# A two-layer decoder step: embeddings split during down, and low halves of gate weights by adding transfers

## Chip, cores and metric

The kernel runs on one core of a Trainium2 chip. The metric is device time of one execution in microseconds (us), as the median of several runs. A profile of one more execution shows where the time goes; times within it count from the start of its span.

## The reference

One inference step of a decoder trunk with two layers, for 512 prompt rows and 8 sample rows (520 columns in all), width 1024. Layer 0 mixes with a short gated convolution, layer 1 with windowed attention on one shared K/V. After the mixer each layer has a feed-forward part and then adds a gated embedding:

```python
hf = rmsnorm(h, norm_ffn_g[i])
h = h + (jax.nn.silu(hf @ ffn_w_gate[i]) * (hf @ ffn_w_up[i])) @ ffn_w_down[i]
gate = jax.nn.sigmoid(rmsnorm(h, norm_ple_g[i]) @ ple_w_gate[i])
h = h + gate * (p[i].astype(h.dtype) @ ple_w_proj[i])
```

Everything is float32. `p[i]` is the layer's embedding input (256 wide), `ple_w_gate` is 1024 x 1024 and `ple_w_proj` 256 x 1024.

## The kernel before

Activations lie feature-major: 8 tiles `h[k]` of 128 features by 520 columns. TensorE multiplies in a fast float format with fewer mantissa bits, so each operand x is split into a high half (ScalarE copies it into that format) and a low half x - high (VectorE subtracts), and each product is three matmuls: high x high, high x low, low x high, on two column halves of 260.

Weights come in raw tiles of 128 x 8 x 128 (512 KB) through SyncE's (SP's) queue into a ring of three raw buffers (`wr`, tag `raw`), in the order of the program. `wsplit` turns each half of a raw tile (four 128-blocks) into a pair of high and low, either in a ring of four pair buffers or in a place given as `dst`. A raw buffer is free when its last reader is done. Where a tile is laid and when an engine takes up an instruction follow from the program order, readiness and free buffers, decided once when the kernel is built; each engine then works in that fixed order.

The feed-forward part (`ffn`) has a plain part of gate and up, then a part in which 2 x 2 blocks are multiplied with seven products instead of eight (`gate_up`, `seven`), then down: a plain part (row blocks m = 0 to 7, 18 weight blocks each, L617 to L628) and a seven-product part (`dd` = 0, 1). In the seven-product parts some low halves are made without VectorE already: `low(..., dma=True)` lets ScalarE write minus the source, rounded to the fast format (that is minus the high half), and a transfer issued on GpSimd's (POOL's) queue adds the source to it (L420 to L424). Down's operands lie in places D7 to D10, DP and X0 to X3, its weight sums in D3 and D4. The two seven-product passes of down end with `after`, which makes squares for the norm (`Norm`) and the operand pairs `px` of the embedding gate: pairs 0 to 3 in D5 and D6, pairs 4 to 7 in X4 to X7. Then the embedding input is loaded and split into `pe` (L649 to L654), in DP.

In layer 0 the gate tiles `pg0{i}` (`dense`, weights through the pair ring) alternate with projection tiles `pj0{m}` (L668 to L682); the norm's factor is finished at `MID` (L670). In layer 1 `last(c, mid)` does the gates and projections once for each column half c. For c = 0 it loads and splits the weights as it goes (`load_last`): projections `wj`, gates 0 and 1 in pair buffers, gates 2 to 7 in D3, D4, D7, D8, D9, D10; for c = 1 they stay there. A gate's bank is freed when VectorE has scaled it by the norm's factor `nq.r` (L1077); that factor comes from a column sum on TensorE, some 13 small VectorE operations (`Norm.start`, `newton_`), a spread by TensorE and a copy by ScalarE (`Norm.spread`, L285). Three banks rotate among gates and projections, and projections lag the gates by two.

Of the kernel before, what the change touches and what calls it, by code (L numbers as in the profile page):

```python
# [10 lines left out]
F32 = mybir.dt.float32  # L11
# [10 lines left out]
T = S + NB  # L22
# [37 lines left out]
def _program(nc, a, o):  # L60
# [3 lines left out]
    with tile.TileContext(nc) as tc, ExitStack() as ctx:  # L64
# [32 lines left out]
        def slot(tag, shape, dt, name):  # L97
            return ap.tile(shape, dt, tag=tag, name=name)
# [30 lines left out]
        def xpair(i, name):  # L129
            t = slot(f"X{i}", [128, 2, T], F32R, name)  # L130
            return t[:, 0, :], t[:, 1, :]
# [20 lines left out]
            V.scalar_tensor_tensor(pair[1], h[k], gain(n, k), pair[0].bitcast(F32), ALU.mult, ALU.subtract)  # L152


        def wsplit(w, name, step=8, dst=None):

            kt = w.shape[1]
            res = []
            for k0 in range(0, kt, step):
                n = min(step, kt - k0)  # L160
                raw = wr.tile([128, 8, 128], F32, tag="raw", name=f"{name}r{k0}")
                nc.sync.dma_start(raw[:, :n], w[:, k0:k0 + n, :])
                for q0 in range(0, n, 4):
                    q = min(4, n - q0)
                    if dst is None:
                        pr = wp.tile([128, 2, 4, 128], F32R, tag="pair", name=f"{name}p{k0 + q0}")
                    else:
                        pr = dst[:, :, k0 + q0:k0 + q0 + q]
                    A.copy(pr[:, 0, :q], raw[:, q0:q0 + q])
                    V.tensor_tensor(pr[:, 1, :q], raw[:, q0:q0 + q], pr[:, 0, :q].bitcast(F32), ALU.subtract)  # L170
                    res += [(pr[:, 0, i, :], pr[:, 1, i, :]) for i in range(q)]
            return res

# [243 lines left out]
            split(4, t4, "D10", True)  # L417
            yield res

        def low(dst, src, hi, dma=False):  # L420

            if dma:
                A.mul(dst, src, -1.0)  # L423
                G.dma_start(out=dst, in_=src, accum_op=ALU.add)  # L424
            else:
                V.tensor_tensor(dst, src, hi.bitcast(F32), ALU.subtract)  # L426

        rings = {"raw": (("raw",) * 3 + ("E0", "E1", "E2"), []), "pair": (("pair",) * 4 + ("E3",), [])}

        def ring(kind, shape, dt, name):  # L430
# [139 lines left out]
        def ffn(i, fx, nf):  # L570

            hid, w = [], {}
            ops = operands(i, nf)
            ahead = weights(a["w_gu"][i], f"{i}", w, ("D3", "DP"), {1: "E4", 3: "E5"})
            plain = [(a[f"w_{n}"][i, m], f"{n[0]}{i}{m}") for m in range(NP) for n in ("gate", "up")]
            mid = [{MID: nf.start}, {4: nf.spread}]
            ws, ps, xs = wsplit(*plain[0]), [], None
            for j in range(2 * NP):
                wn = wsplit(*plain[j + 1]) if j + 1 < 2 * NP else None
                if wn is None:  # L580
                    for _ in range(2):
                        next(ahead)
                ps.append(dense(None, fx, plain[j][1], mid[j] if j < 2 else None, ws))
                ws = wn
                if j % 2:
                    m = j // 2
                    t, u = temp(f"tg{i}{m}"), temp(f"tu{i}{m}")
                    V.tensor_tensor(halves(t), ps[j - 1], halves(nf.r), ALU.mult)
                    A.activation(t, t, AF.Silu)
                    V.tensor_tensor(halves(u), ps[j], halves(nf.r), ALU.mult)  # L590
                    hid.append(cp.tile([128, T], F32, tag=("tabc", "tabs", "k32", "r2")[m], name=f"hid{i}{m}"))
                    V.tensor_tensor(hid[m], t, u, ALU.mult)
                for _ in range((0, 2, 1, 1, 2, 1, 0, 0)[j]):
                    xs = next(ops)
            couples = []
            for d in range(ND):
                if d:
                    t = slot(f"X{d - 1}", [128, 2, T], F32, f"hid{i}d{d}")
                    couples.append(t)
                    out = [t[:, 0], t[:, 1]]  # L600
                else:
                    out = [cp.tile([128, T], F32, tag=tag, name=f"hid{i}{tag}") for tag in ("acc", "r")]
                gate_up(i, d, xs, w, ahead, out)
                hid += out
            hid2, ws = [], []
            for j, tag in enumerate(("D3", "E0", "E1", "E2", "D4", "D5", "D6", "E3", "E4", "E5")):
                if j in (0, 4):
                    ws += wsplit(a["w_down"][i, 0, :, 2 * j:min(2 * j + 8, FP)], f"d{i}0{j}")
                nw = 1 if tag[0] == "E" else 2
                t = slot(tag, [128, nw, 2, T], F32R, f"hid{i}{tag}")  # L610
                for q in range(nw):
                    hid2.append((t[:, q, 0, :], t[:, q, 1, :]))
                    split_to(hid2[-1], hid[len(hid2) - 1])
            ops = inner_operands(i, couples[4:6], couples[6:8])
            w = {}
            ahead = weights(a["w_dd"][i], f"d{i}", w, ("D3", "D4"), {0: "X4", 1: "E4", 3: "E5"})
            for m in range(KD):  # L617
                if m == 2:
                    preload(AF.Sigmoid, h[0])
                if m:  # L620
                    ws = wsplit(a["w_down"][i, m], f"d{i}{m}")
                if m == KD - 1:
                    next(ahead)
                    next(ahead)
                pd = dense(None, hid2, f"d{i}{m}", ws=ws)
                V.tensor_tensor(halves(h[m]), halves(h[m]), pd, ALU.add)
                if m in (2, 4):
                    xs = next(ops)  # L628
            nq = Norm(f"q{i}")
            nid, pairs = (N_PLE0, N_PLE1)[i], []  # L630

            for dd in range(2):
                if dd == 0:
                    for tag in ("D5", "D6"):
                        t = slot(tag, [128, 2, 2, T], F32R, f"px{i}{tag}")
                        pairs += [(t[:, q, 0, :], t[:, q, 1, :]) for q in range(2)]
                else:
                    pairs += [xpair(k, f"px{i}{k}") for k in range(4, KD)]

                def done(x, t, half):  # L640
                    for e in range(2):
                        m = 4 * dd + 2 * e + t
                        c = h[m][:, half * TH:(half + 1) * TH]
                        V.tensor_tensor(c, c, x[:, e], ALU.add)
                        if (t, half) in ((0, 1), (1, 0)):
                            after(m, nq, (nid,), (pairs,))

                seven(f"d{i}", dd, xs, w, ahead, done)
            dp = slot("DP", [128, KP, 2, T], F32R, f"p{i}")  # L649
            pe = [(dp[:, q, 0, :], dp[:, q, 1, :]) for q in range(KP)]  # L650
            for q in range(KP):
                pt = temp(f"pt{i}{q}")
                nc.sync.dma_start(pt, a["pT"][i, :, q, :])
                split_to(pe[q], pt)  # L654
            return pairs, pe, nq

        fx = [xpair(k, f"fx0{k}") for k in range(KD)]
# [9 lines left out]
        pg = {}  # L667
        for i in range(KD + 1):  # L668
            if i < KD:
                pg[i] = dense(a["w_pgate"][0, i], px, f"pg0{i}", {MID: nq.finish} if i == 0 else None)  # L670
                if i == 0:
                    pg[i] = to_sbuf(pg[i], "pg00s")
            m = i - 1
            if m < 0:
                continue
            t = temp(f"tq0{m}")
            V.tensor_tensor(halves(t), pg[m], halves(nq.r), ALU.mult)
            A.activation(t, t, AF.Sigmoid)
            pj = dense(a["w_proj"][0, m], pe, f"pj0{m}")
            V.tensor_tensor(halves(t), pj, halves(t), ALU.mult)  # L680
            V.tensor_tensor(h[m], h[m], t, ALU.add)
            after(m, nk, (N_KV,), (kx,))  # L682
# [358 lines left out]
        def load_last(m):  # L1041
            if m % 2 == 0:
                t = slot(DTAGS[m // 2], [128, 2, 2, KP, 128], F32R, f"wj{m}")
                for q in range(2):
                    wsplit(a["w_proj"][1, m + q], f"wj{m + q}", dst=t[:, q])
                    wj.append([(t[:, q, 0, k], t[:, q, 1, k]) for k in range(KP)])
            if m < 2:
                wg.append(wsplit(a["w_pgate"][1, m], f"wg{m}"))
            else:
                t = slot(("D3", "D4", "D7", "D8", "D9", "D10")[m - 2], [128, 2, KD, 128], F32R, f"wg{m}")  # L1050
                wg.append([(t[:, 0, k], t[:, 1, k]) for k in range(KD)])
                wsplit(a["w_pgate"][1, m], f"wg{m}", dst=t)

        def out_y(ny):
            for k in range(0, KD, 2):
# [139 lines left out]
```

## Time and profile before

| | us |
|---|---|
| median of 3 runs | 1235.31 |
| lowest, highest | 1232.91, 1235.59 |
| the profiled execution | 1235.11 |
| its span | 1233.3 |
| TensorE busy | 1206.2 |
| VectorE busy | 881.1 |
| ScalarE busy | 626.1 |
| GpSimd busy | 106.6 |

The mean granted TensorE clock is 0.99 of full speed. TensorE's instructions overlap, so its busy time says where it had work, and the waits say where it had none. A wait is named by what ended it: the engine, the line and the tile. In the rows a tile's name stands with its number left out where several are alike, and `out<-in` is what an instruction writes and reads.

### The profile page before, as it was taken

What the parts mean: (1) busy time and instruction counts of PE and PEld (TensorE: products, weight loads), DVE (VectorE), ACT (ScalarE), POOL (GpSimd) and SP (SyncE); (2) the same over time, 40 slices, a digit from 0 to 9 for tenths busy, and PEclk for the clock granted to TensorE, in tenths of its full rate; (3) what the DMA queues carried; (4) which work ended last, traced back from release to release, by engine and by line L of the source; (5) the groups of instructions that cost most, each with busy time, mean ns of one, the idle gap of its engine ahead of it and who ended that gap; (6) DMA issues with size and microseconds to landing.
All of it is one profiled execution on the core that took longest, in us unless ns stands there. A gap on an engine that the chain in (4) does not pass through costs nothing.

```text
span 1233.3 us, 23936 instructions
## 1 busy us (share of the span) xinstructions
PE 1206.2 (98%) x9805; PEld 1189.2 (96%) x9805; DVE 881.1 (71%) x1523; ACT 626.1 (51%) x1068; POOL 106.6 (9%) x147
## 2 busy tenths in 40 slices
PE   9999999999999999999998989999999999999896
PEld 8999999999999999999998979999999999999896
DVE  6845557786868853689887777787686779338865
ACT  6322344555555832565544777554555566227531
POOL 2000000101010000100043321000100000001000
PEclk9999999999999999999998999999999999999998
DMA  6223223856565333732431121356656643356312
GB/s 216 87 89 100 89 90 117 206 154 153 155 154 133 83 107 100 204 104 86 146 112 52 41 89 53 117 129 176 154 155 153 159 99 92 94 157 163 108 39 70
DMA packets 56862, 147.59 MB, mean 120 GB/s; under 512 B 5680, under 2 KB 21040, under 8 KB 56752
## 3 DMA queue, kind: packets, MB, share of 16 engines
q1 hardware_dynamic: 47296, 117.66, 30.2%
q0 software_dynamic: 9312, 28.36, 12.4%
q8 instruction: 77, 1.26, 0.4%
q14 instruction: 33, 0.27, 0.1%
q10 hardware_dynamic: 144, 0.03, 0.0%
HBM read 113.10 MB, written 4.58 MB: 95 GB/s over the span
## 4 chain that ended last, share of the span: by engine, by line
PE 88%; DVE 7%; ACT 1%; DMA 1%; issue 1%; POOL 1%; SPq 0%; DVEq 0%; ACTq 0%; POOLq 0%
PE pb L499 13%; PE d L178 13%; PE pd L499 9%; PE pa L499 8%; PE o L178 4%; PE po L178 4%; PE g L178 4%; PE u L178 4%; PE pc L178 3%; PE pg L203 3%; PE pb L178 3%; PE px L178 3%; PE pbd L499 3%; PE pg L178 3%; PE pdd L499 2%; PE pad L499 2%
## 5 line engine op out<-in xcount | busy, mean ns | idle before, releaser
L499 PE MATMUL pb<-xs,wh 128*128 128x260 f32 x864 | 158.9, 283 | 0.0
L499 PEld LDWEIGHTS pb<-xs,wh 128*128 128x128 f32 x864 | 133.4, 188 | 0.0
L426 DVE TENSOR_TENSOR wl<-s,wh 128x1024 fp32r<-128x1024 f32 x72 | 88.1, 1223 | 37.1 <-PE pb L499 27.4
L449 ACT CAST wh<-s 128x1024 fp32r<-128x1024 f32 x72 | 75.7, 1051 | 73.0 <-PE pd L499 53.7
L499 PE MATMUL pd<-xs,wh 128*128 128x260 f32 x576 | 106.9, 286 | 0.0
L499 PE MATMUL pa<-xs,wh 128*128 128x260 f32 x576 | 105.3, 283 | 0.0
L499 PEld LDWEIGHTS pd<-xs,wh 128*128 128x128 f32 x576 | 88.6, 188 | 1.5
L499 PEld LDWEIGHTS pa<-xs,wh 128*128 128x128 f32 x576 | 88.8, 188 | 0.0
L499 PE MATMUL pb<-xs,wl 128*128 128x260 f32 x288 | 81.5, 283 | 0.0
L499 PE MATMUL pd<-xs,wl 128*128 128x260 f32 x288 | 81.4, 283 | 0.0
L499 PEld LDWEIGHTS pd<-xs,wl 128*128 128x128 f32 x288 | 54.2, 188 | 0.0
L499 PEld LDWEIGHTS pb<-xs,wl 128*128 128x128 f32 x288 | 54.2, 188 | 0.0
L499 PE MATMUL pa<-xs,wlE 128*128 128x260 f32 x144 | 40.7, 283 | 0.0
L499 PE MATMUL pa<-xs,wl 128*128 128x260 f32 x144 | 40.7, 283 | 0.0
L499 PE MATMUL pb<-xs,wlE 128*128 128x260 f32 x144 | 40.6, 282 | 0.0
L508 DVE TENSOR_TENSOR u<-pd,u 128x520 f32<-128x520 f32 x36 | 25.0, 695 | 21.7 <-PE pd L499 21.7
L424 POOL DMA_DIRECT2D wlE<-w1r x18 | 15.4, 856 | 228.2 <-ACT wlE L423 228.2
L449 ACT CAST wh<-w3r 128x1024 fp32r<-128x1024 f32 x18 | 18.9, 1052 | 26.9 <-PE pb L499 26.9
L804 ACT ACTIVATE P<-P,nmx 128x256 f32<-128x256 f32 (+1 forms) x64 | 30.2, 474 | 1.4 <-DVE nmx L796 1.1
L449 ACT CAST wh<-w1r 128x1024 fp32r<-128x1024 f32 x18 | 19.0, 1053 | 22.2 <-PE pb L499 22.2
L499 PEld LDWEIGHTS pa<-xs,wlE 128*128 128x128 f32 x144 | 27.2, 189 | 0.0
L499 PEld LDWEIGHTS pb<-xs,wlE 128*128 128x128 f32 x144 | 27.1, 188 | 0.0
(1072 smaller groups left out, 3381.9 us busy)
## 6 DMA issues: line engine op xcount, KB each, us to landing
w1r<-in_w_gu SPq DMA_DIRECT2D x18, 512.0 KB, 3.5
w0r<-in_w_gu SPq DMA_DIRECT2D x18, 512.0 KB, 3.5
w2r<-in_w_gu SPq DMA_DIRECT2D x18, 512.0 KB, 3.5
wlE<-w1r POOLq DMA_DIRECT2D x18, 512.0 KB, 5.5
w3r<-in_w_gu SPq DMA_DIRECT2D x18, 512.0 KB, 3.6
wlE<-w3r POOLq DMA_DIRECT2D x18, 512.0 KB, 4.5
h<-in_xT SPq DMA_DIRECT2D x8, 260.0 KB, 6.0
xs<-xn POOLq DMA_DIRECT2D x4, 520.0 KB, 7.0
```

The lines of the kernel that those rows point to most:

```text
L178: TE.matmul(ps[:, c, :TH], l, r[:, c * TH:(c + 1) * TH], start=(k == 0 and i == 0), stop=(k == len(ws) - 1 and i == 2))
L203: TE.matmul(ps, l, r[:, cols], start=(k == 0 and i == 0), stop=(k == n - 1 and i == 2))
L424: G.dma_start(out=dst, in_=src, accum_op=ALU.add)
L426: V.tensor_tensor(dst, src, hi.bitcast(F32), ALU.subtract)
L449: A.copy(hi, src)
L499: TE.matmul(ps[:, e, :TH], w[l][:, e, k, :], x[r][:, k, :], start=(start and k == 0 and q == 0), stop=(k == 3 and q == 2), skip_group_chec ...
L508: V.tensor_tensor(dst, ps, src, ALU.add)
L804: A.activation(P[:, j, :w], P[:, j, :w], AF.Exp, bias=nmx[:, j:j + 1], accum_out=sm[:, j:j + 1])
```

## The change

The embeddings' input is loaded and split in the plain part of down, after row block m = 5, into places X5 and X6. The gate operands 4 to 7 then lie in D7 (two), X4 and X7. Gate weights 2 to 7 of the last stage move to D8, D9, D10, DP, D3 and D4. `wsplit` gets a list `adder` of the blocks whose low half is made by `low(..., dma=True)`: the second half (blocks 4 to 7) of each gate tile of layer 0, and both halves of gate tiles 2 to 7 of layer 1. `low` itself is moved up unchanged. In layer 0 the call of `wsplit` now stands before the allocation of the gate's bank.

```diff
+        def low(dst, src, hi, dma=False):
+
+            if dma:
+                A.mul(dst, src, -1.0)
+                G.dma_start(out=dst, in_=src, accum_op=ALU.add)
+            else:
+                V.tensor_tensor(dst, src, hi.bitcast(F32), ALU.subtract)
+
+        def wsplit(w, name, step=8, dst=None, adder=()):
...
                     A.copy(pr[:, 0, :q], raw[:, q0:q0 + q])
-                    V.tensor_tensor(pr[:, 1, :q], raw[:, q0:q0 + q], pr[:, 0, :q].bitcast(F32), ALU.subtract)
+                    low(pr[:, 1, :q], raw[:, q0:q0 + q], pr[:, 0, :q], k0 + q0 in adder)
...
                 if m in (2, 4):
                     xs = next(ops)
+                if m == 5:
+                    pe = [xpair(k, f"p{i}{k}") for k in (5, 6)]
+                    for q in range(KP):
+                        pt = temp(f"pt{i}{q}")
+                        nc.sync.dma_start(pt, a["pT"][i, :, q, :])
+                        split_to(pe[q], pt)
             nq = Norm(f"q{i}")
             nid, pairs = (N_PLE0, N_PLE1)[i], []
 
+            def couple(tag, i):
+                t = slot(tag, [128, 2, 2, T], F32R, f"px{i}{tag}")
+                return [(t[:, q, 0, :], t[:, q, 1, :]) for q in range(2)]
+
             for dd in range(2):
                 if dd == 0:
-                    for tag in ("D5", "D6"):
-                        t = slot(tag, [128, 2, 2, T], F32R, f"px{i}{tag}")
-                        pairs += [(t[:, q, 0, :], t[:, q, 1, :]) for q in range(2)]
+                    pairs += couple("D5", i) + couple("D6", i)
                 else:
-                    pairs += [xpair(k, f"px{i}{k}") for k in range(4, KD)]
+                    pairs += couple("D7", i) + [xpair(k, f"px{i}{k}") for k in (4, 7)]
...
                 seven(f"d{i}", dd, xs, w, ahead, done)
-            dp = slot("DP", [128, KP, 2, T], F32R, f"p{i}")
-            pe = [(dp[:, q, 0, :], dp[:, q, 1, :]) for q in range(KP)]
-            for q in range(KP):
-                pt = temp(f"pt{i}{q}")
-                nc.sync.dma_start(pt, a["pT"][i, :, q, :])
-                split_to(pe[q], pt)
             return pairs, pe, nq
...
             if i < KD:
-                pg[i] = dense(a["w_pgate"][0, i], px, f"pg0{i}", {MID: nq.finish} if i == 0 else None)
+                pg[i] = dense(None, px, f"pg0{i}", {MID: nq.finish} if i == 0 else None,
+                              wsplit(a["w_pgate"][0, i], f"pg0{i}", adder=(4,)))
...
             else:
-                t = slot(("D3", "D4", "D7", "D8", "D9", "D10")[m - 2], [128, 2, KD, 128], F32R, f"wg{m}")
+                t = slot(("D8", "D9", "D10", "DP", "D3", "D4")[m - 2], [128, 2, KD, 128], F32R, f"wg{m}")
                 wg.append([(t[:, 0, k], t[:, 1, k]) for k in range(KD)])
-                wsplit(a["w_pgate"][1, m], f"wg{m}", dst=t)
+                wsplit(a["w_pgate"][1, m], f"wg{m}", dst=t, adder=(0, 4))
```

## Rows read from the trace of the kernel before

**Rows 1.** The page: busy us (share of the span) x instructions, all engines.

```profile
PE 1206.2 (98%) x9805; PEld 1189.2 (96%) x9805; DVE 881.1 (71%) x1523; ACT 626.1 (51%) x1068; POOL 106.6 (9%) x147
```

**Rows 2.** Waits of TensorE: line, tile, releaser: us in total, times, longest us.

```profile
PE pj L203 <- DVE tq L1077: 1.9, 1, 1.9
...
PE pg L203 <- DVE s1d L508: 1.2, 1, 1.2
...
PE k L178 <- DVE k1p L170: 0.8, 1, 0.8
...
PE pj L178 <- ACT tq L678: 0.6, 1, 0.6
```

**Rows 3.** Stretches, c=0: length; busy PE, PEld, DVE, ACT, POOL; clock; DMA share.

```profile
1152.40:1189.00 36.60, 33.41 (x262) 32.59 (x261) 28.46 (x70) 19.89 (x45) 0.00 (x0) 0.95 0.37 116
...
1171.60:1174.30 2.70, 2.66 (x12) 2.67 (x13) 2.70 (x7) 2.41 (x7) 0.00 (x0) 0.50 0.17 49
```

**Rows 4.** Timeline of TensorE, c=0: start us, us, instruction, count.

```profile
1157.48 0.76 PE L203 MATMUL pg<-px1D,wg 128*128 128x260 f32 x5
...
1171.64 2.97 PE L203 MATMUL pg<-px1D,wg 128*128 128x260 f32 x12
1174.40 1.75 PE L203 MATMUL pg<-px,wg 128*128 128x260 f32 x12
...
1186.83 2.34 PE L203 MATMUL pj<-p,wj 128*128 128x260 f32 x18
```

**Rows 5.** Timelines of ScalarE and TensorE, layer 0, second half of gate tile 5.

```profile
578.68 0.60 ACT L169 CAST pg05p<-pg05r 128x512 fp32r<-128x512 f32 x1
...
584.83 3.04 PE L178 MATMUL pg<-px,pg05p 128*128 128x260 f32 x24
```

**Rows 6.** Timeline of VectorE: the norm's small operations in layer 1.

```profile
1160.70 0.16 DVE L263 TENSOR_SCALAR n0q<-msq 104x5 f32<-104x5 f32 x1 [0.54 <-PE msq L258]
...
1161.38 0.17 DVE L232 TENSOR_SCALAR n1q<-n0q 104x5 int32<-104x5 int32 x1
...
1165.31 0.17 DVE L235 SCALAR_TENSOR_TENSOR n3q<-n2q 104x5 f32<-104x5 f32 x1
1165.51 0.17 DVE L236 TENSOR_TENSOR n3q<-n3q,n0q 104x5 f32<-104x5 f32 x1
...
1166.12 0.17 DVE L267 TENSOR_TENSOR nrq<-n2q,nrq 104x5 fp32r<-104x5 f32 x1
```

**Rows 7.** Timeline of ScalarE, c=0: gate tiles 2 and 4, the factor's copy.

```profile
1155.78 1.15 ACT L169 CAST wg<-wg2r 128x512 fp32r<-128x512 f32 x2 [1.33 <-DMA wg2r<-in_w_pgate]
...
1168.09 0.62 ACT L169 CAST wg<-wg4r 128x512 fp32r<-128x512 f32 x1 [4.06 <-DMA wg4r<-in_w_pgate]
1168.62 0.65 ACT L285 COPY rq<-rbq 128x416 f32<-128x416 f32 x2
```

**Rows 8.** Timeline of SP's queue: issues of the loads of gate tiles 4 and 6.

```profile
1164.25 0.33 SPq L162 DMA_DIRECT2D wg4r<-in_w_pgate  x1
...
1174.16 0.33 SPq L162 DMA_DIRECT2D wg6r<-in_w_pgate  x1
```

**Rows 9.** The page: DMA queues, packets, MB, share of 16 engines (q0 carries the adds).

```profile
q1 hardware_dynamic: 47296, 117.66, 30.2%
q0 software_dynamic: 9312, 28.36, 12.4%
```

**Rows 10.** The tile wlE's adds (512 KB, 36 of them): issue to landing.

```profile
DMA to landing us min/median/max: 4.5/5.4/9.4
```

**Rows 11.** Transfers of 1127 to 1142 us: size each, us to landing.

```profile
wlE4d<-w1rd POOLq DMA_DIRECT2D x1, 512.0 KB, 8.9
wg1r<-in_w_pgate SPq DMA_DIRECT2D x1, 512.0 KB, 8.4
```

**Rows 12.** The tile p: the embeddings' subtractions, ns min/median/max, first and last start.

```profile
L148 DVE TENSOR_TENSOR p<-pt,p x4: 690/692/693, 554.7 to 1162.8; 128x520 fp32r<-128x520 f32 x4
```

**Rows 13.** ScalarE in 30 us of plain down, layer 1: us, busy (instructions), clock, transfers.

```profile
1070.00:1100.00 30.00, 7.87 (x13) 1.00 0.32 90
```

More of the change, by code (lines that the diff above doesn't have):

```diff
@@ L152, in prep @@
             V.scalar_tensor_tensor(pair[1], h[k], gain(n, k), pair[0].bitcast(F32), ALU.mult, ALU.subtract)
-        def wsplit(w, name, step=8, dst=None):
+        def low(dst, src, hi, dma=False):
[5 more added lines that the diff above has]
+        def wsplit(w, name, step=8, dst=None, adder=()):
             kt = w.shape[1]
@@ L418, in operands @@
             yield res
[L420 to L426, printed above, removed]
         rings = {"raw": (("raw",) * 3 + ("E0", "E1", "E2"), []), "pair": (("pair",) * 4 + ("E3",), [])}
```

## Prediction

> **What bounds the kernel now.** I read the page's busy table first: the matmul engine is busy for 98% of the span [rows 1], so a change can only win what that engine still waits, or the clock it loses by waiting. The second view is therefore who TensorE waited for [rows 2]. Few waits are long, and the change can touch two of them. One, 1.9 us, is in the first column half of the last gates (called c=0 below, 1152.4 to 1189.0 us): the projection's matmuls wait for the gates' scaling by the norm. The other, 0.6 us, is at the same place of layer 0. The 1.2 us on s1d is made by the last additions of down, and the 0.8 us on k1p by keys' weights; neither is touched. The third view is busy time by stretches [rows 3]. In 36.6 us of c=0 PE is busy for 33.4. After the stall (1168.5 to 1170.5) the granted clock stands at 0.50, the 1.2 GHz level, for 2.7 us: twelve matmuls take 2.97 us, and the following twelve 1.75 [rows 4], where 24 take 3.04 at full clock [rows 5]. Of these 4.7 us some 0.3 are a wait for the gates' bank, so the slow clock costs about 1.4 beside the stall itself. Then I read the engines by time around the stall: VectorE [rows 6], ScalarE [rows 7], SyncE's queue [rows 8] and the transfers [rows 9 to 11].
>
> The base: the profiled execution took 1235.1 us, its span 1233.3, so 1.8 lie around it; the median of the three timed runs is 0.2 higher. The sum is made on 1235.1, and 0.2 is added at its end.
>
> **Part 1: the embeddings' split earlier.** Per layer two loads (two SP issues), two ScalarE casts of about 0.6 and two VectorE subtractions of 0.69 [rows 12] leave the stretch in which the norm is finished and go to plain down, behind row block 5. There ScalarE is busy 7.9 of 30 us [rows 13], and the list of PE's waits has none in it. I cost that at nothing. If that cover were gone, it would be the four operations, 2.6 us of two engines in parallel. On SP the two loads now stand ahead of the last weights of plain down and of the first of the seven-product down; they need only temporaries that are long free, so nothing behind them is held. No step of it is on POOL's queue.
> What it wins is seen in the norm's small operations. They depend on one another; two that follow directly start 0.20 us apart [rows 6], but with a weight or embedding subtraction between them the step is 0.68. In layer 1 the chain runs from 1160.70 to 1166.29, 5.6 us, with seven such guests. Two of them are the embeddings'; four more leave by part 3; two steps of wj remain. That leaves about 3.1 us, 2.5 us less. In layer 0 the two embeddings' halves and one or two of the gates' leave a chain of the same kind, about 0.5 us each, so the 0.6 us wait there [rows 2] should go: **-0.6**. Next late behind it is nothing until k1p.
>
> **Part 2: layer 0, upper half of each gate weight by an adding transfer.** Eight VectorE subtractions of 0.69 become eight ScalarE multiplications (a cast of the same shape takes 0.60 [rows 5]) and eight POOL issues of 0.86 us. The trace has no adds under 512 KB; those take 4.5 at the least, 5.4 in the median and 9.4 at most from issue to landing [rows 10]. Their queue moved 28.36 MB in 12.4% of the span on 16 engines [rows 9], 2.8 us for 512 KB; half of it spared leaves 3.1 to 4.0 us for 256 KB, and 8.0 at most. For tile 5 (the others repeat it every 7.2 us): cast at 578.68, multiplication to 579.8, issue 579.9, landed 583.0 to 583.9. PE begins that half at 584.83 [rows 5] and its low part 0.5 us later. **Cost 0**, cover 1.4 us; one landing of 8.0 would cost 2.6. The raw tile is freed some 3 us later, and the next load stands behind it on SP, but pj05r lies 6 us ahead of its use.
>
> **Part 3: layer 1, both halves of gate weights 2 to 7 by adding transfers.** Other places: D8 to D10 are free no later than D3 and D4 were, and the loads wait for raw buffers and not for places, so **0**. The adds take 12 subtractions from VectorE and put 12 multiplications on ScalarE and 12 issues on POOL, idle here. Bounded by the same rows each low half is ready 0.5 + 0.5 + 0.1 + (3.1 to 4.0) after its raw tile, where before it was about 1.7. I follow PE.
> At 1157.48 PE does five matmuls of tile 2 [rows 4] while the second pair of operands is made. Tile 2's raw data are there at 1155.78 [rows 7]; its low half will be at 1160.1 to 1161, so this work comes later and PE has nothing else: gates 0 to 2 end near 1165.2, not 1163.6. The two multiplications may also stand before the norm's squares, which costs that chain 1.0 us at most. The norm's chain ends 1.5 to 2.5 earlier all the same. If the copy of the norm factor is then ahead of the cast of tile 4 on ScalarE (in before it stood behind it, and that cast waited for its load until 1168.09 [rows 7]), the stall of 1.9 and the slow clock are gone: pj1 ends at 1170.5, not 1171.2.
> Tile 4: its load was issued at 1164.25 [rows 8], when tile 3's buffer came free. That one now waits for adds, to about 1166, but wj4's frees at about 1163 (its cast follows tile 3's four operations on ScalarE, which begin near 1160), so I take 1163. Low halves 1170.3 to 1172: gate 4 ends 1173.4 to 1174.9 against 1176.0. Tile 6 takes tile 4's buffer at about 1172, two us earlier than 1174.16 [rows 8], but its lows need 8 us from the issue, not 5: first half 1179.6 to 1182.0. PE would want it at 1177.7 to 1179.2, and waits. Gate 7 ends 1186.1 to 1188.6; before, 1186.83 [rows 4]. So what is won at the stall is paid back to the raw buffers, each of which a gate tile now holds 9 to 10 us instead of 5.5. At a landing time of 3.3, nearer to the quiet bound because nothing but loads is beside the adds, gate 7 ends at 1186.7: **-0.1**, between -0.7 and +1.8. From 1189 on all weights lie ready, and nothing changes.
>
> The Trainium skill, DMA: Bandwidth & Descriptors, section "Anatomy of one DMA — SWDGE (gpsimd) path", gives 2.0 us plus the bytes over 436 GB/s for a DMA issued from GpSimd, an estimate of 3.2 us for 512 KB and 2.6 for 256 KB. The quickest 512 KB add here took 4.5, so the rows decide; with 2.6 gate 7 would end near 1184.7 and the sum be 1232.6.
>
> **The sum.** 1235.1 - 0.6 (layer 0) - 0.1 (c=0) = 1234.4; on the median's footing **1234.6**, no change that can be told: a measurement of this kernel can tell about 0.2%, 2.5 us.
>
> **The rivals.**
> Faster, the supply keeps up: adds land in under 3 us, or the buffers rotate better than I reckoned (a gate tile takes the first free one). Then all of the stall goes: 0.6 + 1.9 + 0.3 (gate 4's own wait behind it) + 1.4 of slow clock = 4.2 at most, and 1231 to 1232.7. For it: POOL's queue is empty there, ScalarE is busy for only half of c=0, the norm chain surely shortens. Against it: the three raw buffers.
> Slower, the transfers fill the DMA engines: gate tiles 2 to 7 and four projections are 3.7 MB of loads, at the loads' 117.66 MB in 30.2% of the span (316 GB/s) [rows 9] 11.6 us; the adds are 3.1 MB at 2.8 us per 512 KB, 17 us. Together 28.6 us of all 16 engines in a stage that has some 28 before tile 7 must be there; in before the share was 0.37 [rows 3]. A load and an add of 512 KB that were in flight together took 8.4 and 8.9 us [rows 11]. With 6 us landings each of the two turns (tile 2 or 3 to 4, 4 to 6) slips by 2 to 3 us, gate 7 ends 3 to 5 us later than now, and a long wait brings the low clock again: 1238 to 1240. It decides from a landing above about 5 us.
> The Trainium skill, DMA: Bandwidth & Descriptors, section "Queues, rings and completion order", says that a DMA engine alternates between the queues that have work, packet by packet. The two that were in flight together agree with it.
> No effect at all of part 3, because ScalarE still keeps the factor's copy behind tile 4's cast: the stall is then about as long, and the time 1234.5 to 1236; it counts with the forecast.
>
> **How the numbers follow.** Forecast (with the last case) 0.42, faster 0.36, slower 0.22; the chances of within 0.2%, faster and slower by more than that are the same three. The forecast's own range is 1233.5 to 1236.8. The whole range takes in the faster case but for its last tenth and the slower but for its upper third: 1231 to 1238.6.
>
> **What would show it.** Right: no subtractions of embeddings inside the norm's chain, that chain near 3 us; no wait of pj on tq in either layer; a new PE wait on an adding transfer of tile 4 to 7, and POOL issues spaced by the raw buffers. Wrong: adds of 256 KB that land in under 3 or over 5 us; tile 6 issued before 1171 or after 1175 (on before's clock); a granted clock of 0.50 in c=0 at another place; new waits on adds between 566 and 605 us. The prediction fails as a whole if the order in which engines take up the casts shifts in stages that I hold untouched, above all at the start of the seven-product down.

## The result and the profile after

The changed kernel takes 1243.23 us in the median of six runs (1241.53 to 1244.95), the kernel before 1235.45 beside it; the ratio is 1.0066, 95% interval 1.0053 to 1.0079. It is slower, where no change was forecast, and it lies above the range. The profiled execution of after took 1242.39 us, its span 1240.6. (After's lines stand 9 further down than before's, from L162 to L420: the pair product L203 is L212; from there on 1 to 9 further; in the kernels of the experiments they differ by up to 2 more. `low` is L158, ScalarE, L159, the adding transfer, and L161, VectorE's subtraction.)

All of the loss is in one stretch, the first column half of the last gates (c=0), which is 45.6 us long instead of 36.6 [rows 3]. It begins 1.9 us earlier than before (1150.51, not 1152.40), so times within it are compared from its start. The stretches of after, first the whole of c=0, then two parts of it; columns as in [rows 3]:

```profile
1150.51:1196.06 45.55, 36.19 (x262) 33.18 (x261) 21.55 (x57) 24.90 (x54) 10.30 (x12) 0.96 0.67 151
1167.40:1171.20 3.80, 3.47 (x18) 3.17 (x19) 1.20 (x3) 3.12 (x7) 0.54 (x1) 0.66 0.40 71
1178.80:1182.20 3.40, 1.70 (x12) 1.49 (x12) 0.43 (x1) 0.52 (x2) 0.00 (x0) 1.00 0.89 225
```

VectorE is relieved there, from 28.5 us to 21.6, as the change intends, and TensorE idles 9.4 us instead of 3.2. That is 6.2 of the 9.0 us; in the other 2.8 TensorE counts as busy for longer, in part at the lower clock (second row; 0.50 from 1169.0 to 1171.0), and what else is in them was not parted. Who it waited for, after:

```profile
PE pg L212 <- DMA wg<-wg5r: 2.6, 2, 1.7
PE pg L212 <- DMA wg<-wg3r: 2.4, 1, 2.4
PE pg L212 <- DMA wg<-wg7r: 1.0, 2, 0.6
PE pj L212 <- DVE tq L1089: 0.5, 1, 0.5
PE pg L212 <- DMA wg<-wg4r: 0.4, 1, 0.4
PE pg L212 <- DMA wg<-wg6r: 0.4, 1, 0.4
```

The wait of 1.9 on the norm's factor [rows 2] is gone. In its place are 6.8 us of waits on adding transfers, most of them those of tiles 3, 5 and 7. Why just these is seen on SyncE's queue, in the issues of the loads of gate tiles 2 to 7, after:

```profile
1150.45 0.33 SPq L171 DMA_DIRECT2D wg2r<-in_w_pgate  x1
1153.95 0.33 SPq L171 DMA_DIRECT2D wg3r<-in_w_pgate  x1
1163.02 0.33 SPq L171 DMA_DIRECT2D wg4r<-in_w_pgate  x1
1169.88 0.33 SPq L171 DMA_DIRECT2D wg5r<-in_w_pgate  x1
1177.06 0.46 SPq L171 DMA_DIRECT2D wg6r<-in_w_pgate  x1
1182.22 0.33 SPq L171 DMA_DIRECT2D wg7r<-in_w_pgate  x1
```

The same of before, of which the prediction read only tiles 4 and 6 [rows 8]; here are 5 and 7:

```profile
1164.68 1.63 SPq L162 DMA_DIRECT2D wg5r<-in_w_pgate  x1
...
1174.92 0.33 SPq L162 DMA_DIRECT2D wg7r<-in_w_pgate  x1
```

Before, the loads come in pairs: 4 and 5 within 0.4 us, 6 and 7 within 0.8, and a pair 9.9 us after the other. After, from tile 4 on, they come singly, every 5 to 7 us. The last load is issued 22.5 us into c=0 before and 31.7 us into it after, 9.2 later, and c=0 ends 14.1 and 13.8 us behind that load. So c=0 has grown by about as much as its last load has slipped: in after the supply of raw tiles sets its length, which the experiments below test. The chain of waits of after names the transfers of that supply (start, us):

```profile
1162.53 7.30 DMA wg<-wg3r
...
1169.88 3.56 DMA wg5r<-in_w_pgate
...
1176.57 5.60 DMA wg<-wg5r
...
1188.33 4.85 DMA wg<-wg7r
```

Tile 3's second add lands at 1169.83, and 0.05 us later tile 5's load is issued into the buffer that this add frees; tile 5's second add lands at 1182.17, and tile 7's load follows at 1182.22. One turn of the buffer is 12.3 us.

Outside c=0 the profiled execution is 1.7 us shorter. In layer 0 the gates and projections took 58.2 us from their first matmul to the start of the last projection, and 57.3 after. The wait of 0.6 there [rows 2] is gone, and no wait on an add has come. The rest is mostly in stages that the change leaves alone: layer 0's gates start 1.6 us later (547.0, not 545.4), and the attention of layer 1, from the keys' first matmul to the start of the queries' last, takes 153.6 us instead of 155.8. In the kernels of this case that attention stretch takes 152.6 to 155.9 us, so differences of 2 to 3 us there say nothing about a change.

### The profile page after: what moved, and what is told of

Same layout as the page of the kernel before. It is cut to its first block, busy times and chain, and to the rows that moved or that the text cites. A ratio compares the mean times of both kernels' runs of the same rounds, so it can differ in the third digit from the quotient of the medians.

```text
span 1240.6 us, 23992 instructions
## 1 busy us (share of the span) xinstructions
PE 1206.9 (97%) x9805; PEld 1187.5 (96%) x9805; DVE 872.2 (70%) x1503; ACT 636.4 (51%) x1088; POOL 124.4 (10%) x167
## 4 chain that ended last, share of the span: by engine, by line
PE 44%; DVE 6%; DMA 2%; ACT 2%; issue 1%; POOL 1%; DVEq 0%; POOLq 0%; SPq 0%; ACTq 0%
PE d L187 6%; PE pb L500 6%; PE pd L500 4%; PE pa L500 4%; PE o L187 4%; PE pg L187 3%; PE pg L212 2%; PE g L187 2%; PE u L187 2%; PE q L187 1%; PE pbd L500 1%; PE av L842 1%; PE pt L829 1%; PE pdd L500 1%; PE s L791 1%
## 5 line engine op out<-in xcount | busy, mean ns | idle before, releaser
L161 DVE TENSOR_TENSOR wl<-s,wh 128x1024 fp32r<-128x1024 f32 x72 | 88.1, 1223 | 37.5 <-PE pb L500 27.8
L500 PE MATMUL pa<-xs,wlE 128*128 128x260 f32 x144 | 40.7, 283 | 0.0
L500 PE MATMUL pa<-xs,wl 128*128 128x260 f32 x144 | 40.7, 283 | 0.0
L212 PE MATMUL pg<-px1D,wg 128*128 128x260 f32 x216 | 31.8, 294 | 7.0 <-DMA wg<-wg5r 2.6
L159 POOL DMA_DIRECT2D wlE<-w1r x18 | 15.4, 857 | 229.4 <-ACT wlE L158 229.4
L212 PEld LDWEIGHTS pg<-px1D,wg 128*128 128x128 f32 x216 | 28.2, 193 | 9.0 <-DMA wg<-wg3r 3.1
```

Source lines behind the costliest of these rows:

```text
L212: TE.matmul(ps, l, r[:, cols], start=(k == 0 and i == 0), stop=(k == n - 1 and i == 2))
L500: TE.matmul(ps[:, e, :TH], w[l][:, e, k, :], x[r][:, k, :], start=(start and k == 0 and q == 0), stop=(k == 3 and q == 2), skip_group_chec ...
```

## The experiments

Every kernel ran beside the kernel before on the same chip; ratios are to that. Before's own median beside them is 1233.4 to 1235.5, so ratios compare better than medians. In the diffs of the last weights, `LW` stands for `wsplit(a["w_pgate"][1, m], f"wg{m}", dst=t`.

**No adds in the last weights** (after without part 3):

```diff
-LW, adder=(0, 4))
+LW)
```

> The changed kernel, but VectorE again makes the low halves of the last gate weights (layer 1, tiles 2 to 7); the early split of the embeddings, the new places and the adds of layer 0 stay. Theory A (the loss is made by the adding transfers of the last gates, which hold the raw buffers): the last gates' first half c=0 falls from 45.6 us to under 36.6, since the embeddings' two subtractions are out of the norm's chain; with the 0.9 us won in layer 0 the time is 1231.5 to 1235. Theory B (the loss comes from the moved places or the early split): 1241 to 1244, c=0 near 45.

Measured: 1231.09 us, ratio 0.9971 (0.996 to 0.9982), 0.4 below theory A's band. The loss is gone, and the rest of the change is faster than before. c=0 is 34.6 us long:

```profile
1149.94:1184.52 34.58, 31.96 (x263) 31.23 (x261) 27.20 (x69) 18.63 (x43) 0.00 (x0) 1.00 0.32 107
```

**Only the adds in the last weights** (before with part 3 alone, in before's places):

```diff
-LW)
+LW, adder=(0, 4))
```

> The kernel before, with one thing of the change: both low halves of the last gate tiles 2 to 7 by adding transfers. Theory A: c=0 is 44 to 47 us and the time 1242 to 1246, a little worse than the changed kernel, since the gains of the other parts are missing. Theory B: 1234 to 1237.

Measured: 1246.39 us, ratio 1.0091 (1.0078 to 1.0105); c=0 is 49.3 us long, with waits of 3.1 on tile 5's adds, 2.8 on tile 3's and 1.5 on tile 7's. Time and stretch lie a little above theory A's bands, far from theory B's. So the loss belongs to part 3 by itself, in the old places too.

**Raw places of their own** (after, with gate tiles 2 to 7 not in the ring of three but each in a place that is free there):

```diff
-        def wsplit(w, name, step=8, dst=None, adder=()):
+        def wsplit(w, name, step=8, dst=None, adder=(), own=None):
...
-                raw = wr.tile([128, 8, 128], F32, tag="raw", name=f"{name}r{k0}")
+                raw = (slot(own, [128, 8, 128], F32, f"{name}r{k0}") if own else
+                       wr.tile([128, 8, 128], F32, tag="raw", name=f"{name}r{k0}"))
...
-LW, adder=(0, 4))
+LW, adder=(0, 4),
+   own=("E0", "E1", "X0", "X1", "X2", "X3")[m - 2])
```

> The changed kernel, but the raw tiles of gates 2 to 7 of layer 1 go to places of their own (E0, E1, X0 to X3, all free by then) instead of the ring of three, so that no load waits for an add. Theory A1 (it is the turn of the raw buffers: add lands, next load starts, next add): the loads start by 1151 us and all low halves are there in time, c=0 is 33 to 36.5 us, the time 1230 to 1234. Theory A2 (it is the throughput of the DMA engines, or the landing time of the adds themselves): the adds land at 5 to 9 us each in a bunch, c=0 stays over 39 and the time over 1237.

Measured: 1231.1 us, ratio 0.9975 (0.9962 to 0.9988). The same twelve adds, four of them (tiles 2 and 3) now ahead of c=0, and no wait of TensorE on any of them. The stretch of c=0:

```profile
1151.06:1184.22 33.16, 31.91 (x262) 31.20 (x261) 21.34 (x56) 20.41 (x47) 6.88 (x8) 1.00 0.57 139
```

All gate loads are issued by 1151.85, and the adds still take 3.3, 4.1 and 6.1 us (least, median, most). What decides is thus how early a raw tile can be loaded. That it isn't the throughput of the DMA engines is seen beside the kernel with two places (below): it too has eight adds in c=0 and a DMA share of 0.55, against 0.57 here, and yet its c=0 takes 39.0 us.

**Half of the adds** (after with the second halves only):

```diff
-LW, adder=(0, 4))
+LW, adder=(4,))
```

> The changed kernel, but only the second half of each of the last gate tiles 2 to 7 has its low part by an adding transfer, as in layer 0; VectorE makes the first. Theory A1 (turns of the raw buffers): each tile still waits for one add, so a turn (load, cast, multiplication, add) shortens only by what the second add queues behind the first, 1 to 2 us of some 12; c=0 is 39 to 44 us, the time 1237 to 1242. Theory A2 (the moved bytes count): half the bytes, half the loss or less, 1235 to 1238.5.

Measured: 1234.59 us, ratio 0.9996 (0.9988 to 1.0005), c=0 38.9 us. This is below the bands of both theories, of theory A2's by 0.4 us; its "half the loss or less" holds. By the ratios half of the adds carry 2.5 of the 9.5 thousandths that lie between the first experiment (0.9971) and after (1.0066), about a quarter. The trace shows where it comes from. The adds' landing and two loads in this kernel:

```profile
DMA to landing us min/median/max: 3.3/3.7/4.3
```

```profile
1162.56 0.38 SPq L171 DMA_DIRECT2D wg4r<-in_w_pgate  x1
1165.84 0.33 SPq L171 DMA_DIRECT2D wg5r<-in_w_pgate  x1
```

With one add a tile in flight, tile 3's lands in 4.3 us where the second one of after took 7.3, and was issued 1 us earlier; tile 5's load comes at 1165.84 instead of 1169.88. So the landing time counts as a term of the turn, and it depends on what is in flight.

**Raw places, no adds** (the kernel with raw places of their own, without `adder` in the last weights):

```diff
-LW, adder=(0, 4),
+LW,
```

> The kernel after, the last gate weights 2 to 7 with raw tiles in places of their own and no adding transfers. With raw places free, 1231.1 stood with the adds (e3_own_raw), and without adds but in the ring also 1231.1 (e1_no_adds_last). Theory T (the raw buffers' turns are the whole cost of the adds, and the adds by themselves neither win nor lose): 1230 to 1232, the same as both, c=0 33 to 35 us. Rival U (the adds win something when buffers are free, and the ring costs something also without them): the two effects come apart here: VectorE's subtractions back in c=0 with free buffers give 1232.5 or more if the adds win, 1229.5 or less if the ring cost something without adds.

Measured: 1234.28 us, ratio 0.9995 (0.9981 to 1.0009), so rival U holds in its first half. With buffers free, the kernel with the adds (0.9975) is ahead of this one. The intervals just overlap; the traces tell the two apart, 33.2 us of c=0 against 36.5. VectorE in layer 1's norm, the first and last of the small operations, with two of their ten guests:

```profile
1161.06 0.17 DVE L273 TENSOR_SCALAR n0q<-msq 104x5 f32<-104x5 f32 x1 [0.63 <-PE msq L268]
...
1164.39 0.68 DVE L161 TENSOR_TENSOR wg<-wg6r,wg 128x512 fp32r<-128x512 f32 x1
...
1166.42 0.68 DVE L161 TENSOR_TENSOR wg<-wg7r,wg 128x512 fp32r<-128x512 f32 x1
...
1167.62 0.17 DVE L277 TENSOR_TENSOR nrq<-n2q,nrq 104x5 fp32r<-104x5 f32 x1
```

The early weights bring even tiles 6 and 7 into the norm's chain, which lasts 6.7 us (with the adds in these places 3.1). PE's wait of 1.5 on the scaling is back, and c=0 takes 36.5 us, as before. So what the adds win with free buffers is what the early loads cost without them: against the first experiment, with the ring and no adds (0.9971), the kernel with free buffers and all adds (0.9975) wins nothing.

**The early split alone** (after with no `adder` anywhere) and **layer 0's adds alone** (before with part 2):

```diff
-LW, adder=(0, 4))
+LW)
...
-wsplit(a["w_pgate"][0, i], f"pg0{i}", adder=(4,))
+wsplit(a["w_pgate"][0, i], f"pg0{i}")
```

> The kernel after without any adding transfer for gate weights: only the early split of the embeddings and the new places are left. Theory P (the gain of e1_no_adds_last, 3.6 us, is the early split: the norm's chain is 2 to 3 us shorter in both layers, so the stall of 1.9 and the slow clock of 1.4 in layer 1 and the 0.6 in layer 0 go): 1230.5 to 1232.2. Rival Q (the adds of layer 0 carry part of it: without them the wait of 0.6 is back and the seven products behind layer 0 start later): 1232.3 to 1234, and a wait of PE on tq in layer 0 of 0.4 us or more.

```diff
-pg[i] = dense(a["w_pgate"][0, i], px, f"pg0{i}", {MID: nq.finish} if i == 0 else None)
+pg[i] = dense(None, px, f"pg0{i}", {MID: nq.finish} if i == 0 else None,
+              wsplit(a["w_pgate"][0, i], f"pg0{i}", adder=(4,)))
```

> The kernel before with the upper half of layer 0's gate weights by adding transfers, and nothing else of the change. Theory P (the early split carries the gain): the same as before within 0.7 us, 1234 to 1235.5, PE's wait of 1.9 us in layer 1 still there, that of 0.6 in layer 0 between 0 and 0.6. Rival Q: 1232 to 1233.9.

Measured: 1231.47, ratio 0.9976 (0.9963 to 0.9989), and 1235.05, ratio 1.0005 (0.9992 to 1.0018). The early split, with its new places, carries the whole gain; layer 0's adds carry none that can be told. No run has the new places without the split. In the kernel with the split alone, layer 1's waits on the scaling and the stretch of c=0:

```profile
PE pg L212 <- DVE tq L1089: 0.6, 1, 0.6
...
PE pj L212 <- DVE tq L1081: 0.2, 1, 0.2
```

```profile
1150.09:1183.90 33.81, 31.84 (x262) 31.09 (x261) 27.16 (x68) 18.92 (x43) 0.00 (x0) 1.00 0.34 110
```

c=0 is 2.8 us shorter than before, and layer 0's wait of 0.6 is gone, together 3.4 by the traces; the medians differ by 3.2. Of the 2.8 us, 1.2 are less idle time of TensorE and 1.6 less busy time, at a clock of 1.00 instead of 0.95. The norm's chain is only 1.0 us shorter (4.6). The other part is a load: without the embeddings' two subtractions VectorE is done with tile 3 sooner, so tile 4 is loaded 10.4 us into c=0 instead of 11.9, and ScalarE, where the factor's copy still stands behind tile 4's cast, does that cast at 13.9 instead of 15.7:

```profile
1160.50 0.33 SPq L171 DMA_DIRECT2D wg4r<-in_w_pgate  x1
```

```profile
1164.02 0.62 ACT L178 CAST wg<-wg4r 128x512 fp32r<-128x512 f32 x1 [2.40 <-DMA wg4r<-in_w_pgate]
1164.54 0.64 ACT L294 COPY rq<-rbq 128x416 f32<-128x416 f32 x2
```

With layer 0's adds alone that wait stays:

```profile
PE pj L186 <- ACT tq L679: 0.7, 1, 0.7
```

**One raw place more, and two** (after, tile 5, then tiles 3 and 5 in places of their own):

```diff
-LW, adder=(0, 4))
+LW, adder=(0, 4),
+   own="E0" if m == 5 else None)
```

> The kernel after with one raw tile more: gate tile 5 of layer 1 loads into a place of its own, so that it no longer waits for tile 3's buffer and tile 7 can have that one. All adds stay, 12 in the last stage. Theory A1 (the turn of the buffers 3 to 5 to 7, some 12 us each, is the cost): the waits on wg5r (2.6) and wg7r (1.0) go with the slow clock behind them, the wait on wg3r (2.4) may stay: 1236 to 1239, c=0 38 to 42 us. Rival A2 (the adds land too slowly when loads are beside them, whatever buffer they hold): the adds and loads are as many, 1241 to 1244.

```diff
-LW, adder=(0, 4))
+LW, adder=(0, 4),
+   own={3: "E1", 5: "E0"}.get(m))
```

> The kernel after with two raw tiles more, for gate tiles 3 and 5 of layer 1; e8_own_tile5 had one (1239.15, PE's waits 2.1 on wg3r and 1.2 on wg4r), e3_own_raw six (1231.1, none). All adds stay. Theory A1 (the turns): the wait on wg3r goes, since tile 3 is then loaded before 1150; tile 4 still waits for tile 2's buffer: c=0 35 to 38.5 us, 1233 to 1236.5. Rival A2 (landing beside loads): nothing is won against one place more, 1238 to 1240.

Measured: 1239.15, ratio 1.0036 (1.0023 to 1.0049), c=0 40.7 us; and 1234.9, ratio 1.0007 (0.9994 to 1.002), c=0 39.0 us. So with none, one, two and six places the ratio is 1.0066, 1.0036, 1.0007 and 0.9975. The first median is 0.15 above its band, and in the second c=0 is longer than expected though the time is as expected: each kernel shows which turn is left. With one place it is tile 3's adds (first row), with two tile 4's (second and third row):

```profile
PE pg L213 <- DMA wg<-wg3r: 2.1, 1, 2.1
```

```profile
PE pg L213 <- DMA wg<-wg4r: 2.9, 2, 2.5
...
1167.77 5.88 DMA wg<-wg4r
```

Tile 4's load does wait for a buffer, but not for tile 2's, as was expected: it takes that of the projection tile wj4, as soon as VectorE has subtracted there, between two steps of the norm:

```profile
1159.69 0.42 DVE L161 TENSOR_TENSOR wj<-wj4r,wj 128x256 fp32r<-128x256 f32 x1
```

```profile
1160.14 0.33 SPq L172 DMA_DIRECT2D wg4r<-in_w_pgate  x1
```

And while tile 4's second add is under way, the loads of tiles 6 and 7 start at 1168.25 and 1168.67. The add takes 5.9 us; at the quickest add's 3.3 it would have landed 2.6 us earlier, and the wait is 2.5. So in this kernel the late load and the shared landing make the wait together, and these runs don't part them further.

**Raw places, and adds for tiles 4 to 7 only:**

```diff
-LW, adder=(0, 4),
+LW, adder=(0, 4) if m >= 4 else (),
```

(from the kernel with six raw places)

> As e3_own_raw (raw tiles of gate weights 2 to 7 in places of their own), but the adding transfers only for tiles 4 to 7; the low halves of tiles 2 and 3 are VectorE's again. Theory G (VectorE's subtractions cost only as guests between the norm's small operations, and with their raw tiles in hand at 1147 those of tiles 2 and 3 are done before that chain begins; ScalarE has four multiplications less ahead of the norm's squares): the chain stays at 3 to 3.5 us, PE's wait of 1.1 on ScalarE's px1D shrinks below 0.5, 1229.8 to 1231.1. Rival H (the subtractions of tiles 2 and 3 slip into the chain, or the sums of down behind them come later): the chain is 4.5 us or more, or PE waits 0.5 or more on VectorE in that stretch: 1231.5 to 1233.5.

Measured: 1228.25 us, ratio 0.9951 (0.9935 to 0.9968), the fastest of all, faster than both kernels of the case and below theory G's band. c=0:

```profile
1148.70:1181.05 32.35, 31.93 (x262) 31.22 (x261) 21.60 (x57) 20.61 (x48) 6.85 (x8) 1.00 0.58 139
```

TensorE idles 0.4 us in it. The wait on ScalarE's px1D fell from 1.1 (six places, all adds) to 0.2, and the norm's chain stays at 3.1 us, as theory G said. That makes 0.8 of the gain on the version with all adds; the medians differ by more (0.9951 against 0.9975), but their intervals overlap. The profiled executions differ by 3.9 us, and 3.0 of these are in the attention of layer 1 (152.7 against 155.7 us), which the edit doesn't touch. The interval also overlaps that of the first experiment, so that this kernel beats the ring without adds isn't shown.

## Why the prediction was wrong

**Part 1 (cost 0, chain 3.1, layer 0 by 0.6): right.** The chain in after runs from 1158.94 to 1161.73, 2.8 us, against 5.6 before [rows 6], and its thirteen steps stand 0.2 apart:

```profile
1158.94 0.17 DVE L272 TENSOR_SCALAR n0q<-msq 104x5 f32<-104x5 f32 x1 [0.62 <-PE msq L267]
1159.13 0.17 DVE L241 TENSOR_SCALAR n1q<-n0q 104x5 int32<-104x5 int32 x1
...
1161.56 0.17 DVE L276 TENSOR_TENSOR nrq<-n2q,nrq 104x5 fp32r<-104x5 f32 x1
```

Layer 0 won 0.9. One count in the working is off: it names seven guests and then disposes of eight, since part 3 takes three and not four (one half of tile 2, two of tile 3); in after the two of wj come behind the chain too. With the split alone the chain is 4.6 us, and with tile 4's earlier load that already ends most of the stall and the slow clock of layer 1. What the prediction left out is that part 1 needs no part 3 for this: taking out the two embeddings' guests wins 2.8 us of c=0.

**Part 2 (cost 0): right.** The adds of layer 0's tiles 0, 1, 2 and 5 land in 3.3, 5.5, 3.3 and 3.5 us, no wait follows, and the run with part 2 alone is level.

**Part 3 (-0.1, between -0.7 and +1.8): wrong**, by some 9 us in c=0. The stall and its slow clock went, as said, and the norm factor's copy is ahead of tile 4's cast. Two steps failed. (The prediction's times are those of before, where c=0 begins 1.9 us later than in after.)

The first is the term for a gate tile's time in its buffer. Tile 4 was reckoned from a load at 1163 to low halves at 1170.3 to 1172, 10.6 to 19.6 us into c=0. The load came at 1163.02, 12.5 us into c=0, and the second half's low near 1176.1, 25.6 us into it. The three parts in after:

```profile
1168.68 0.62 ACT L178 CAST wg<-wg4r 128x512 fp32r<-128x512 f32 x1 [0.23 <-DMA wg4r<-in_w_pgate]
```

```profile
1170.66 0.86 POOL L159 DMA_DIRECT2D wg<-wg4r  x1 [7.28 <-ACT wg L158]
1171.70 0.86 POOL L159 DMA_DIRECT2D wg<-wg4r  x1 [0.18 <-issue]
```

```profile
wg4r<-in_w_pgate SPq DMA_DIRECT2D x1, 512.0 KB, 5.6
...
wg<-wg4r POOLq DMA_DIRECT2D x2, 256.0 KB, 4.4
```

The load took 5.6 us, where it took 3.8 before (issue 1164.25 [rows 8], cast 1168.09 [rows 7]): tile 3's adds were in flight. From the cast to the second add's issue it was 3.0, where the prediction counted 1.1 for one half and left out that the buffer waits for both, and that other work of ScalarE stands between. The two adds landed in 4.4 in the median, not 3.3. Sum 13.1 from load to landing, against the 9 to 10 that the prediction gave a buffer. Nor was a buffer held for only 5.5 us before: from issue to the last reader's end tiles 2 to 6 held theirs for 9.1, 8.3, 6.8, 9.5 and 5.9 us, and in after for 11.6, 15.9, 13.1, 12.3 and 11.9. The landing over all twelve, in after:

```profile
DMA to landing us min/median/max: 3.3/4.4/7.3
```

The value of 3.3 that was taken is the least of these. It was argued that nothing but loads would be beside the adds. But loads and adds that are in flight together are both longer (7.3 here, beside two loads and the tile's first add), and so are the two adds of one tile: tile 7's second took 4.85 after the last load had landed, beside its first.

The second step is a chain that the sum doesn't follow: tile 3's buffer on to tiles 5 and 7. Before, tile 4 took tile 3's buffer (1164.25) and tile 5 that of wj4 (1164.68). After, tile 4 takes wj4's, as reckoned, and so tile 3's falls to tile 5. The prediction let tile 3's buffer wait for adds "to about 1166", 13.6 us into c=0; it was held to 1169.83, 19.3 us into it, with tile 3's second add 7.3 us under way beside the loads of wj5 and tile 4. It then went on with tiles 4 and 6 and not with this buffer; and tile 6 didn't get tile 4's buffer either, which went to wj7 at 1176.39, but wj6's, at 1177.06, 26.6 us into c=0 and not 19.6. Tile 5 held tile 3's buffer for 12.3 us more, and tile 7, loaded at 1182.22, has its last low half at 1188.33 + 4.85 = 1193.2, 42.7 us into c=0, where the forecast had gate 7 done 33.7 to 36.2 us into it. The run with one place for tile 5 shows what this chain is worth: 3.0 thousandths of the time, of the 9.5 that lie between the first experiment and after.

Three of the prediction's signs of being wrong came: landings over 5 us, tile 6 issued after 1175 (1179.0 on before's clock) and a clock of 0.50 at another place in c=0 (1169.0 to 1171.0). Of its signs of being right, a wait of 0.5 of pj on tq is left, late in c=0.

The Trainium skill, DMA: Bandwidth & Descriptors, section "Anatomy of one DMA — SWDGE (gpsimd) path", gives an estimate of 2.6 us for 256 KB, which the trace does not bear out: no add took less than 3.2. The Trainium skill, DMA: Bandwidth & Descriptors, section "Queues, rings and completion order", says that a DMA engine takes the packets of its busy queues in turn, and with that the traces agree: loads and adds that overlap are both longer, though they don't show single packets.

**The rivals.** The slower one had the right sign and the right mechanism in part: each turn slips, from landings beside loads. Its price was too low (1238 to 1240): it gave each turn a slip of 2 to 3 us on the same tiles 4 and 6, where tile 3's buffer slipped by 5.7 against the forecast and its next turn by another 2 to 3, with a slow clock from 1169.0 besides. Its point, a landing above 5 us, isn't reached by the median (4.4), but by two of the three adds on the chain of waits (7.3, 5.6 and 4.85); the third is just below it. And its first argument, the DMA engines' throughput, falls: in after their share of c=0 is 0.67, and with places of their own the adds don't hold TensorE at all. The faster rival's sum (4.2 less, 1231 to 1232.7) is what came when buffers were free (1231.1), but its adds under 3 us did not come, and the runs without adds in layer 1 are as fast (1231.09 and 1231.47).

## What to carry to other kernels

An adding transfer that reads a raw buffer holds that buffer until it lands; before one replaces a subtraction, take the time from load to landing for every tile of the ring, with loads and adds in flight together, and follow every buffer to the end of the stage, with the small tiles that take a turn in it too. Moving work off a busy engine pays only where that engine stands on the path: here in a dependent chain of 0.2 us steps, in which each unrelated operation that happens to be ready costs up to half a microsecond, and in the raw tiles that the engine frees sooner. When loads come earlier, ask what becomes ready and slips into such a chain.

## What was not expected of the hardware

A transfer of 128 KB took 5.6 us in after, beside two adds and a load of 512 KB, where the same kind took 2.0 in a quiet stretch:

```profile
wj2r<-in_w_proj SPq DMA_DIRECT2D x1, 128.0 KB, 2.0
...
wj5r<-in_w_proj SPq DMA_DIRECT2D x1, 128.0 KB, 5.6
```

The granted clock doesn't follow the length of a wait alone. In after it stood at 0.66 in the mean over the 3.8 us behind the wait of 2.39: 0.87 up to 1169.0, 0.50, the 1.2 GHz level, from there to 1171.0, and 1.00 from 1172.1 on. But behind a wait of 2.14 in the kernel with one place more, and behind one of 1.67 in after, the four matmuls that follow take 0.75 us at a clock of 1.00, where the four behind a wait of 2.54 in the kernel with two places took 0.98:

```profile
1167.58 3.52 PE L212 MATMUL pg<-px1D,wg 128*128 128x260 f32 x16 [2.39 <-DMA wg<-wg3r]
...
1182.21 0.74 PE L212 MATMUL pg<-px1D,wg 128*128 128x260 f32 x4 [1.67 <-DMA wg<-wg5r]
```

```profile
1169.51 0.75 PE L213 MATMUL pg<-px1D,wg 128*128 128x260 f32 x4 [2.14 <-DMA wg<-wg3r]
```

```profile
1173.69 0.98 PE L213 MATMUL pg<-px1D,wg 128*128 128x260 f32 x4 [2.54 <-DMA wg<-wg4r]
```

Before, a stall of 1.92 was enough [rows 3]. What parts these cases was not tried.
